# One step of a four-layer streaming encoder on one core: five plain column blocks per feed-forward, and full-height low parts of the attention queries

## The chip, the core and the metric

The kernel runs on one core of a Trainium2 chip. The metric is the device time of one execution in microseconds (us). Five engines work side by side, each on its own list of instructions: PE (TensorE, matmuls; PEld is its weight load), DVE (VectorE), ACT (ScalarE), POOL (GpSimd) and SP (which only issues DMAs here). The scheduler inside the kernel fixes the order on each engine when the program is built, so an engine waits when the next instruction on its list is not ready.

## The reference, cut to what matters

Four layers run over 576 tokens at once (512 of a prompt, 64 of a running stream), model width 1024. Each layer adds a token mixer (pool, delta rule, stick-breaking attention, pool) and then a feed-forward; this is the feed-forward and the part of attention in which the queries are used:

```python
def _conv_ffn(h, buf, w_up, conv_w, conv_b, w_down):      # D_FF = 2816
    val, gate = jnp.split(h @ w_up, 2, axis=-1)
    gate, new_buf = _causal_dwconv(gate, buf, conv_w)
    return (jax.nn.silu(gate + conv_b) * val) @ w_down, new_buf

def _sb_attend(q, k, v, q_pos, k_pos):                    # 16 heads of 64
    z = jnp.einsum('bqhd,bshd->bhqs', q, k).astype(jnp.float32) * (SB_DH ** -0.5)
    mask = k_pos[None, :] < q_pos[:, None]
    log_1m = jnp.where(mask, jax.nn.log_sigmoid(-z), 0.0)
    rest = lax.cumsum(log_1m, axis=3, reverse=True) - log_1m
    a = jnp.where(mask, jnp.exp(jax.nn.log_sigmoid(z) + rest), 0.0)
    return jnp.einsum('bqhs,bshd->bqhd', a, v.astype(jnp.float32))
```

## The kernel before, in words

**Precision.** Every 32-bit matrix is split into a rounded high part (written by ACT) and a low part, the rest (written by DVE). A product is three matmuls: high by high, high weight by low token, low weight by high token. The tokens' parts are `xh[m]`, `xl[m]` for m = 0 to 7 (128 features by 576 tokens each); weights pass from raw tiles `r` to split tiles `h` (8 of them).

**Stages.** P0 F0 D1 F1 S2 F2 P3 F3 and an ending: mixer, then feed-forward, of each layer. In the trace F0 begins near 70 us, F1 near 935, S2 near 1304, F2 near 1678, F3 near 2120.

**A feed-forward (`ffn`)** has 22 column blocks j of 128. The first `J0` (4) are plain: `up(j)` makes gate and value, each 8 k-steps by 3 products by 2 token halves of 288, so 96 matmuls of 288 columns. The others, `up2(j)`, make gate and value together as a 2 by 2 block product by seven products instead of eight (84 matmuls of 288 columns). The seven products take other operands: the tokens already normalised (`xh`, `xl` rewritten in place), and sums of token quarters, `T`. `sums(k)`, for k = 0 to 3, makes both: on DVE two multiplications, four subtractions and three low parts give T of k; then, once the event `plain` has fired (after the last plain block's matmuls), ACT rewrites `xh[k]`, `xh[k+4]` (rows `xh<-b`) and DVE `xl[k]`, `xl[k+4]` (rows `xl<-b,xh`). Block J0 waits for all four k before its first product. `splitter2` makes the seven weight combinations on DVE (rows `r<-r`) and splits them (`h<-r,h`). `down(js)` multiplies a group of finished blocks into the residual `x`: 96 matmuls for the first group of two blocks (0, 1), 192 for a group of four; its results are added by DVE (`a<-p,a`, two per output tile m). The first group's `down` is put after block `max(2, J0-1)`, thus after the last plain block and ahead of the first seven-product block.

**Attention (`sb`)**: per pair of heads `q_post` scales the queries into `t`, then writes two tiles `qa[e]` (e = 0, 1 for the two heads; the rounded queries of one head, twice, on both partition halves) and one tile `qb` (each head's low part on its own 64 partitions). The keys `k_[e]` hold a head's rounded part on its own half and its low part on the other, so one matmul over 128 partitions gives (high + low key) by high query (`sc`). Then the mask is added by bf16 matmuls against `idb` (`diag`), and `half` adds high key by low query over 64 partitions alone. Per head `attend` does this for three score tiles in the order 1, 2, 0: tile 1 has low matmuls of 384 and 128 columns, tile 2 of 256, 64, 64 and 64, tile 0 of 512. That is 7 per head, 112 in all.

**The scheduler** (`Flow.run`) is a list of generators with priorities: it always emits the next step of the most urgent one whose operands are ready by its own clocks, and keeps each engine's list in that order. Pools bound it: 25 tiles `a`, 8 `b`, 11 `d` (128 by 128, mostly for the delta rule's chain).

Of the kernel before, what the change touches and what calls it, by code (L numbers as in the profile page):

```python
# [9 lines left out]
F32 = mybir.dt.float32  # L10
F32R = mybir.dt.float32r
BF16 = mybir.dt.bfloat16
AF = mybir.ActivationFunctionType
ALU = mybir.AluOpType
# [3 lines left out]
class Eng:  # L18

    def __init__(self, flow, name, obj):  # L20
        self.flow, self.name, self.obj = flow, name, obj
# [268 lines left out]
class Step:  # L290
    def __init__(self, ctx, tc, I, O):
        self.tc=tc; nc=self.nc=tc.nc; self.I=I; self.O=O; self.n=0
        f=self.f=Flow(tc)
        self.V,self.A,self.G,self.E,self.S=f.V,f.A,f.G,f.E,f.S
        self.cp=ctx.enter_context(tc.tile_pool(name="const",bufs=1))
        self.sp=ctx.enter_context(tc.tile_pool(name="sb",bufs=1))
        self.dp=ctx.enter_context(tc.tile_pool(name="dr",bufs=1,space=bass.MemoryType.DRAM))
        self.pp=ctx.enter_context(tc.tile_pool(name="ps",bufs=1,space=PSUM))
        for tag,n in (("a",25),("b",8),("r",4),("h",8),("p",8),("q",8),("d",11)): f.slots(tag,n)
        f.slots("so",1); f.slots("t",8)  # L300
        f.lim.update(w=8,g=4,c=8,z=3,o=2,f=6)
        self.jobs=[]; self.specs=[]; self.wq={}; self.spl=[]; self.ngot=0
        self.x=[None]*KD; self.xd={}; self.rb={}; self.acc={}; self.cnt=Counter()
# [341 lines left out]
    def ffn(self,l,st,nst,gnext):  # L645
# [3 lines left out]
        cw,fst=self.fc[l]; gb=32+8*l  # L649
        act={}; ps={}  # L650
        so=[None]
        J0=4
        def conv(j,Gt,c):
            yield [Gt,"@A"]
            A.activation(c[:,:578],Gt[:,2:580],AF.Identity,bias=cw[:,66+j:67+j],scale=cw[:,44+j:45+j])
            G.tensor_copy(so[0][:,0:2,j],Gt[:,512:514]); G.tensor_copy(so[0][:,2:4,j],Gt[:,578:580])
            yield [c,"@V"]
            V.scalar_tensor_tensor(out=c[:,:578],in0=Gt[:,1:579],scalar=cw[:,22+j:23+j],in1=c[:,:578],op0=ALU.mult,op1=ALU.add)
            V.scalar_tensor_tensor(out=c[:,:578],in0=Gt[:,0:578],scalar=cw[:,j:j+1],in1=c[:,:578],op0=ALU.mult,op1=ALU.add)
# [41 lines left out]
        def up(j,stag):  # L701
            def gen():
                if j==0:
                    f.lim["g"]=6
                    yield [("so",1)]
                    so[0]=self.s([128,4,NF],F32,"so",1)
                f.spawn(post(j),10)
                need=self.xneed(st) if j==0 else None
                if stag:
                    W=[]  # L710
                    for i in (0,1): W.append((yield from self.wget()))
                    P=[[None,None],[None,None]]; ps[j,0],ps[j,1]=P
                    for h in (0,1):
                        for i in (0,1):
                            yield [("p",1,"g")]
                            P[i][h]=self.p("g")
                            yield from self.gemm(P[i],W[i][0],0,self.xk,KD,halves=(h,),need=need)
                            if h: f.free(*W[i][1])
                            f.fire(f"{st}:{'gv'[i]}{j}:{h}")
                else:  # L720
                    for i in (0,1):
                        w,hl=yield from self.wget()
                        yield [("p",2,"g")]
                        P=[self.p("g"),self.p("g")]; ps[j,i]=P
                        yield from self.gemm(P,w,0,self.xk,KD,need=need)
                        f.free(*hl)
                        for h in (0,1): f.fire(f"{st}:{'gv'[i]}{j}:{h}")
                if j==J0-1: f.fire(f"{st}:plain")
            self.job(gen,(wu[:,:,DFF+128*j:DFF+128*j+128],KD,128),(wu[:,:,128*j:128*j+128],KD,128))
# [48 lines left out]
        def frees():  # L778
            yield [f"{st}:N{k}" for k in range(4)]+[f"{st}:post{j}" for j in range(J0)]
            f.free(self.rb[st])  # L780
# [5 lines left out]
        def tok(i,k):  # L786
            if i in (1,2,4): return T[i,k][:,H0],T[i,k][:,H1]
            m,h=((k,H0),(k+4,H0),(k+4,H1),(k,H1))[(11,21,22,3).index(i)]
            return self.xh[m][:,h],self.xl[m][:,h]
# [38 lines left out]
        def up2(j):  # L828
            def gen():
                B=[None]*3  # L830
                f.spawn(post2(j,B),10)
                for n,(b,t,read) in enumerate(SEQ):
                    w,hl=yield from self.wget()
                    if read: yield [f"{st}:{read}{j}"]
                    start=B[b] is None
                    if start:
                        yield [("p",1,"g")]
                        B[b]=self.p("g")
                    o=B[b][:,:HW]
                    for k in range(4):  # L840
                        if j==J0: yield [f"{st}:{'T' if t in (1,2,4) else 'N'}{k}"]
                        xh,xl=tok(t,k)
                        yield [xh,xl]
                        wh,wl=w[0][:,k],w[1][:,k]

                        mm(o,wh,xh,start=start and k==0,stop=False,skip_group_check=not start)
                        mm(o,wh,xl,start=False,stop=False,skip_group_check=not start)
                        mm(o,wl,xh,start=False,stop=k==3,skip_group_check=not start)
                    f.free(*hl)
                    f.fire(f"{st}:P{j}:{n}")  # L850
                if j==NF-1: f.free(*T.values())
            self.job(gen,(wu[:,:,DFF+128*j:DFF+128*j+128],wu[:,:,128*j:128*j+128]))
# [48 lines left out]
        for g in groups:  # L901
            for j in g:
                if j<J0: up(j,j==0)
                else: up2(j)
                if pend is not None and j==max(g[0],J0-1): down(pend,False); pend=None
            pend=g
# [775 lines left out]
    def sb(self,l,st,nst,gnext):  # L1682
# [60 lines left out]
        HS=(slice(0,64),slice(64,128))  # L1743
# [3 lines left out]
        def q_post(p_,P):  # L1747
            rb=self.rb[st]
            yield [f"{st}:rb0",f"{st}:rb1",("a",1)]
            t=self.a()  # L1750
            for h in (0,1):
                a,b=HALF[h]
                yield [P[h][:,:HW],rb[:,a:b],"@V"]
                V.scalar_tensor_tensor(out=t[:,a:b],in0=P[h][:,:HW],scalar=0.125,in1=rb[:,a:b],op0=ALU.mult,op1=ALU.mult)
                f.free(P[h])
            yield [t,("a",3),"@A"]
            qa=[self.a(F32R),self.a(F32R)]; qb=self.a(F32R)
            for e in (0,1):
                for r in (e,1-e): A.activation(qa[e][HS[r],:NT],t[HS[e],:NT],AF.Copy)
            for e in (0,1):  # L1760
                yield [qa[e],"@V"]
                V.tensor_tensor(out=qb[HS[e],:NT],in0=t[HS[e],:NT],in1=qa[e][HS[e],:NT].bitcast(F32),op=ALU.subtract)
            f.free(t)
            qT[p_]=(qa,qb)
            f.fire(f"{st}:q{p_}")
# [42 lines left out]
        def proj(which,p_):  # L1808
            def gen():
                w,hl=yield from self.wget()  # L1810
                yield [("p",2,"g")]
                P=[self.p("g"),self.p("g")]
                yield from self.gemm(P,w,0,self.xk,KD)
                f.free(*hl)
                f.spawn((q_post,k_post)[which](p_,P),TN[('pc','pd')[which]])
            self.job(gen,(W[:,:,1024*which+128*p_:1024*which+128*p_+128],KD,128))
# [4 lines left out]
        def attend(p_,e):  # L1821
            n_=2*p_+e
            yield [f"{st}:q{p_}",f"{st}:k{p_}"]+([f"{st}:z{n_-1}"] if n_ else [])
            (qa,qb),k_,kp=qT[p_],kT[p_],kP[p_]
            hs=HS[e]; z={}; E={}; X={}; Lt={}

            def sc(*parts):
                for n,(o,kk,qs) in enumerate(parts): mm(o,kk,qa[e][:,qs],start=n==0,stop=False)
            def half(*parts):
                for n,(o,kk,qs) in enumerate(parts): mm(o,kk[hs],qb[hs,qs],start=False,stop=n==len(parts)-1)  # L1830
            def zk(b):
                i,c,n=reg[b]
                return z[i][:,c:c+n],k_[e][:,128*b:128*b+128],slice(128*b,512)
# [35 lines left out]
            def post(i):  # L1869
# [7 lines left out]
                if not left[0]:  # L1877
                    EE[p_,e]=E
                    f.fire(f"{st}:E{p_}:{e}")
            yield [qa[e],qb[hs,:NT],k_[e],kp[:,:512],self.idb,self.mkb,self.ntri,self.none]  # L1880
            for i in order:
                yield [("p",1,"z")]
                z[i]=self.p("z")
# [7 lines left out]
                half(*ps)  # L1891
                f.spawn(pre(i),TN['pe'])
            f.fire(f"{st}:z{n_}")
            if e: f.free(*qa,qb,*k_,kp)
            def Lr(b,x):
                i,c,n=reg[b]
                return X[i][x][:,c:c+n]
# [47 lines left out]
        q=lambda p_: proj(0,p_)  # L1945
        for x in TN['order2'].split(): dict(k=k,q=q,v=values)[x[0]](int(x[1:]))
        for p_ in range(8):
            for e in (0,1): f.spawn(attend(p_,e),TN['pa'])
            f.spawn(av(p_),TN['pb'])
# [88 lines left out]
```

## Time and profile before

| what | value |
|---|---|
| median of 3 runs | 2518.58 us (2518.18 to 2522.79) |
| the profiled execution, its own time | 2525.03 us |
| its span, first to last instruction | 2523.3 us |
| mean granted TensorE clock | 0.986 of full speed |
| PE busy | 2462.4 us (98%), 18337 matmuls |
| DVE, ACT, POOL busy | 1924.9 us (76%), 1298.2 us (51%), 365.9 us (15%) |

The span is nearly all PE time, so the table is read by what keeps PE from its next matmul, and by how fast it does each one. Matmuls overlap: a row's duration runs from the matmul's start to its end, and the pace is the distance from one start to the next.

### The profile page before, as it was taken

How to read it: one execution, taken by the hardware profiler on the slowest of the kernel's cores; microseconds unless marked ns; L12 is line 12 of the kernel's file. 1: busy time of each engine (PE TensorE's matmuls, PEld its weight loads, DVE VectorE, ACT ScalarE, POOL GpSimd, SP SyncE). 2: the span in 40 equal slices, each digit the busy share in tenths (PEclk: the TensorE clock that was granted, in tenths of full speed). 3: DMA queues.
4: the chain of work that ended last, by engine and by line, in shares of the span. 5: the costliest groups of instructions: out<-in, count | busy, mean ns of one | idle time of the engine just before them, and what ended most of it. 6: DMA issues, size and time to landing. Idle time of an engine off the chain costs nothing.

```text
span 2523.3 us, 46793 instructions
## 1 busy us (share of the span) xinstructions
PE 2462.4 (98%) x18337; PEld 2394.3 (95%) x18337; DVE 1924.9 (76%) x3727; ACT 1298.2 (51%) x2459; POOL 365.9 (15%) x734
## 2 busy tenths in 40 slices
PE   8989999998999999999999999999999999899998
PEld 7989999998999899999999888899999999899998
DVE  6988787887555479877885767779777788877776
ACT  6455544544344344444565667645444465544445
POOL 0000000138441001000001221200000001000000
PEclk9999999999999999999999999999999999999999
DMA  3223223332322222323233122222233231223231
GB/s 110 83 87 101 84 78 100 108 95 62 79 65 57 75 77 63 97 88 97 86 125 113 51 78 64 92 71 79 84 91 94 86 107 53 76 76 97 88 95 62
DMA packets 349056, 212.91 MB, mean 84 GB/s; under 512 B 30298, under 2 KB 341210, under 8 KB 348836
## 3 DMA queue, kind: packets, MB, share of 16 engines
q1 hardware_dynamic: 348836, 209.93, 28.3%
q8 instruction: 144, 2.36, 0.4%
q14 instruction: 76, 0.62, 0.1%
HBM read 192.41 MB, written 17.47 MB: 83 GB/s over the span
## 4 chain that ended last, share of the span: by engine, by line
PE 66%; DVE 2%; issue 1%; ACT 0%; POOL 0%; DVEq 0%; POOLq 0%; ACTq 0%
PE p L26 66%; DVE a L26 1%; DVE h L26 1%; DVE r L26 0%; ACT a L26 0%; DVE b L26 0%; ACT b L26 0%; POOL t L26 0%; DVE xl L26 0%; DVE q L26 0%; ACT xh L26 0%; DVEq L2034 0%; ACT q L26 0%; POOL rtf L26 0%; POOLq L2034 0%
## 5 line engine op out<-in xcount | busy, mean ns | idle before, releaser
L26 PE MATMUL p<-xh,h 128*128 128x288 f32 x4864 | 1040.6, 300 | 24.1 <-ACT xh L26 20.9
L26 PEld LDWEIGHTS p<-xh,h 128*128 128x128 f32 x4864 | 803.6, 189 | 31.1 <-ACT xh L26 22.2
L26 ACT ACTIVATE h<-r 128x512 fp32r<-128x512 f32 (+1 forms) x708 | 508.4, 739 | 420.1 <-PE p L26 320.9
L26 PE MATMUL p<-xl,h 128*128 128x288 f32 x2432 | 706.0, 297 | 1.6 <-DVE xl L26 1.6
L26 PE MATMUL p<-b,h 128*128 128x288 f32 x4992 | 681.0, 297 | 5.6 <-ACT b L26 3.0
L26 PEld LDWEIGHTS p<-b,h 128*128 128x128 f32 x4992 | 668.5, 189 | 9.3 <-DVE b L26 3.8
L26 DVE TENSOR_TENSOR h<-r,h 128x512 fp32r<-128x512 f32 (+1 forms) x708 | 580.7, 829 | 52.4 <-ACT h L26 51.3
L26 PEld LDWEIGHTS p<-xl,h 128*128 128x128 f32 x2432 | 461.6, 190 | 3.5 <-DVE xl L26 3.2
L26 DVE TENSOR_TENSOR a<-p,a 128x288 f32<-128x288 f32 (+6 forms) x650 | 265.8, 448 | 197.8 <-PE p L26 188.6
L26 PE MATMUL p<-a,h 128*128 128x288 f32 x2592 | 374.1, 299 | 0.0
L26 PEld LDWEIGHTS p<-a,h 128*128 128x128 f32 x2592 | 359.5, 192 | 0.0
L26 POOL COPY so<-a 128x2 f32<-128x2 f32 x176 | 100.2, 599 | 1513.5 <-DVE a L26 1513.5
L26 ACT ACTIVATE a<-a 128x512 f32<-128x512 f32 (+6 forms) x362 | 192.9, 555 | 133.8 <-DVE a L26 117.3
L26 ACT ACTIVATE q<-p 128x288 f32<-128x288 f32 x288 | 118.2, 410 | 185.3 <-PE p L26 181.5
L26 DVE SCALAR_TENSOR_TENSOR a<-a,fcw,a 128x578 f32<-128x578 f32 x176 | 144.2, 819 | 5.5
L26 DVE TENSOR_TENSOR a<-p,q 128x288 f32<-128x288 f32 (+2 forms) x216 | 70.5, 355 | 53.7 <-PE p L26 53.5
L26 ACT ACTIVATE b<-a 128x576 fp32r<-128x576 f32 x96 | 65.5, 682 | 81.7 <-DVE a L26 81.5
L26 POOL TENSOR_TENSOR a<-a,a 128x512 fp32r<-128x512 f32 (+1 forms) x64 | 67.3, 1052 | 252.5 <-DVE a L26 237.5
L26 DVE TENSOR_TENSOR r<-r 128x512 f32<-128x512 f32 x144 | 99.9, 694 | 4.3
L26 PE MATMUL p<-a,a 128*128 128x128 f32 (+10 forms) x656 | 102.8, 287 | 0.1
L26 ACT ACTIVATE xh<-a,gains 128x288 fp32r<-128x288 f32 (+2 forms) x128 | 66.3, 531 | 70.8 <-DVE a L26 70.3
L26 DVE TENSOR_TENSOR r<-r,r 128x512 f32<-128x512 f32 x144 | 99.0, 688 | 2.5
(192 smaller groups left out, 2424.7 us busy)
## 6 DMA issues: line engine op xcount, KB each, us to landing
r<-in_ffn_w_up_dram SPq DMA_DIRECT2D x176, 512.0 KB
r<-in_ffn_w_down_dram SPq DMA_DIRECT2D x80, 512.0 KB
r<-in_dn_w_in_dram SPq DMA_DIRECT2D x32, 512.0 KB
r<-in_sb_w_qkv_dram SPq DMA_DIRECT2D x24, 512.0 KB
d<-a SPq DMA_DIRECT2D x24, 288.0 KB
a<-d SPq DMA_DIRECT2D x16, 288.0 KB
r<-in_ffn_w_down_dram SPq DMA_DIRECT2D x16, 256.0 KB
r<-in_dn_w_out_dram SPq DMA_DIRECT2D x8, 512.0 KB
```

The lines of the kernel that those rows point to most:

```text
L26: r = f(*a, **k)
```

## The change

`J0` becomes 5: block 4 of each feed-forward is plain instead of seven-product, and `down` of blocks 0 and 1 moves behind it. `qb` becomes a tile per head: 64 partitions of zeros (a memset on POOL), and the low part on the other 64; `half` then runs over all 128 partitions against the whole `k_[e]`. `q_post` asks for four `a` tiles at once instead of three. The pool of `a` grows by one, that of `d` shrinks by three.

```diff
-        for tag,n in (("a",25),("b",8),("r",4),("h",8),("p",8),("q",8),("d",11)): f.slots(tag,n)
+        for tag,n in (("a",26),("b",8),("r",4),("h",8),("p",8),("q",8),("d",8)): f.slots(tag,n)
...
-        J0=4
+        J0=5
...
-            yield [t,("a",3),"@A"]
-            qa=[self.a(F32R),self.a(F32R)]; qb=self.a(F32R)
+            yield [t,("a",4),"@A"]
+            qa=[self.a(F32R),self.a(F32R)]; qb=[self.a(F32R),self.a(F32R)]
+            for e in (0,1): G.memset(qb[e][HS[1-e],:NT].bitcast(F32),0.0)
...
-                V.tensor_tensor(out=qb[HS[e],:NT],in0=t[HS[e],:NT],in1=qa[e][HS[e],:NT].bitcast(F32),op=ALU.subtract)
+                V.tensor_tensor(out=qb[e][HS[e],:NT],in0=t[HS[e],:NT],in1=qa[e][HS[e],:NT].bitcast(F32),op=ALU.subtract)
...
-                for n,(o,kk,qs) in enumerate(parts): mm(o,kk[hs],qb[hs,qs],start=False,stop=n==len(parts)-1)
+                for n,(o,kk,qs) in enumerate(parts): mm(o,kk,qb[e][:,qs],start=False,stop=n==len(parts)-1)
...
-            yield [qa[e],qb[hs,:NT],k_[e],kp[:,:512],self.idb,self.mkb,self.ntri,self.none]
+            yield [qa[e],qb[e][:,:NT],k_[e],kp[:,:512],self.idb,self.mkb,self.ntri,self.none]
...
-            if e: f.free(*qa,qb,*k_,kp)
+            if e: f.free(*qa,*qb,*k_,kp)
```

The change also moves instructions. On DVE in F0, before, around the start of the first seven-product block (`xl<-b,xh` are the rewritten tokens; b_953 and b_954 belong to k = 2 and 3, `q` and `a` to T of k = 3, h_1629 to weights):

```order
L26 TENSOR_TENSOR h_1629<-r_1421,h_1629 128x512
L26 TENSOR_TENSOR xl_81<-b_953,xh_73 128x576
L26 TENSOR_TENSOR xl_85<-b_953,xh_77 128x576
L26 TENSOR_TENSOR q_1380<-b_954 128x288
L26 TENSOR_TENSOR q_1648<-b_954,q_1380 128x288
L26 TENSOR_TENSOR a_1646<-q_1380,a_1646 128x288
L26 TENSOR_TENSOR q_1653<-b_954,q_1648 128x288
L26 TENSOR_TENSOR b_954<-b_954 128x288
L26 TENSOR_TENSOR a_1650<-q_1648,a_1650 128x288
L26 TENSOR_TENSOR a_1655<-q_1653,a_1655 128x288
L26 TENSOR_TENSOR xl_82<-b_954,xh_74 128x576
L26 TENSOR_TENSOR xl_86<-b_954,xh_78 128x576
```

These twelve stood behind all sixteen additions of `down` of blocks 0 and 1. On DVE in F0 of the change, the same place (a_1530 is block 4, a_101 the residual's tile 0):

```order
L26 TENSOR_TENSOR a_1530<-a_1529,a_547 128x512
L26 TENSOR_TENSOR a_1530<-a_1529,a_547 128x64
L26 TENSOR_TENSOR xl_79<-b_951,xh_71 128x576
L26 TENSOR_TENSOR xl_83<-b_951,xh_75 128x576
L26 TENSOR_TENSOR xl_80<-b_952,xh_72 128x576
L26 TENSOR_TENSOR xl_84<-b_952,xh_76 128x576
L26 TENSOR_TENSOR xl_81<-b_953,xh_73 128x576
L26 TENSOR_TENSOR xl_85<-b_953,xh_77 128x576
L26 TENSOR_TENSOR xl_82<-b_954,xh_74 128x576
L26 TENSOR_TENSOR xl_86<-b_954,xh_78 128x576
L26 TENSOR_TENSOR a_101<-p_1606,a_101 128x288
L26 TENSOR_TENSOR a_101<-p_1607,a_101 128x288
```

All eight rewritten low parts now stand together ahead of the first addition of that `down`, and T of k = 3 ahead of them; the same holds in F1, F2 and F3. On DVE of the change, some 15 rows further on, where `down` ends and the first seven-product block begins (a_107, a_108 are the residual's tiles 6 and 7; r_1409 and r_1480 the raw weights of block 5; h_1646, h_1756 and h_1774 the low parts of its products 0, 6 and 1):

```order
L26 TENSOR_TENSOR a_107<-p_1723,a_107 128x288
L26 TENSOR_TENSOR a_107<-p_1724,a_107 128x288
L26 TENSOR_TENSOR h_1646<-r_1409,h_1646 128x512
L26 TENSOR_TENSOR h_1756<-r_1480,h_1756 128x512
L26 TENSOR_TENSOR r_1480<-r_1480 128x512
L26 TENSOR_TENSOR a_108<-p_1739,a_108 128x288
L26 TENSOR_TENSOR r_1480<-r_1409,r_1480 128x512
L26 TENSOR_TENSOR r_1409<-r_1480,r_1409 128x512
L26 TENSOR_TENSOR h_1774<-r_1480,h_1774 128x512
```

The first low parts of the new block's weights now stand behind the additions of tiles 6 and 7.

## Rows read from the trace of the kernel before

**Rows 1.** Busy time in stretches: stretch, length, PE, PEld, DVE, ACT, POOL, clock, DMA.
```profile
70.00:131.00 61.00, 59.47 (x444) 59.13 (x442) 56.09 (x109) 26.68 (x42) 5.25 (x16) 1.00 0.26 78
...
994.00:1304.00 310.00, 309.27 (x2319) 308.95 (x2319) 250.02 (x443) 157.37 (x288) 27.66 (x70) 0.99 0.32 96
...
1480.00:1626.00 146.00, 144.80 (x1048) 127.30 (x1047) 105.44 (x180) 99.70 (x170) 36.72 (x37) 0.99 0.25 77
```

**Rows 2.** PE's waits: for whom, us in total, times, longest.
```profile
PE p L26 <- ACT xh L26: 20.9, 5, 8.5
...
PE p L26 <- DVE xl L26: 1.6, 5, 0.8
```

**Rows 3.** DVE in order of time, transitions of F0 and F1: start, us, instruction.
```profile
134.53 1.42 DVE L26 TENSOR_TENSOR xl<-b,xh 128x576 fp32r<-128x576 f32 x2
...
138.77 1.43 DVE L26 TENSOR_TENSOR xl<-b,xh 128x576 fp32r<-128x576 f32 x2
...
976.93 3.43 DVE L26 TENSOR_TENSOR xl<-b,xh 128x576 fp32r<-128x576 f32 x5
```

**Rows 4.** Groups of instructions on DVE: count, busy us, mean ns, idle before.
```profile
L26 DVE TENSOR_TENSOR h<-r,h 128x512 fp32r<-128x512 f32 x520 | 350.2, 685 | 41.1 <-ACT h L26 41.1
...
L26 DVE TENSOR_TENSOR h<-r,h 128x1024 fp32r<-128x1024 f32 x188 | 230.5, 1228 | 11.3 <-ACT h L26 10.2
L26 DVE TENSOR_TENSOR a<-p,a 128x288 f32<-128x288 f32 x488 | 203.9, 453 | 182.1 <-PE p L26 179.3
...
L26 DVE SCALAR_TENSOR_TENSOR a<-a,fcw,a 128x578 f32<-128x578 f32 x176 | 144.2, 819 | 5.5
...
L26 DVE TENSOR_TENSOR r<-r 128x512 f32<-128x512 f32 x144 | 99.9, 694 | 4.3
```

**Rows 5.** Busy time in stretches, as in rows 1: six falls of the clock.
```profile
133.60:143.80 10.20, 6.28 (x21) 5.29 (x22) 8.80 (x17) 4.77 (x11) 0.00 (x0) 0.50 0.36 104
993.70:997.20 3.50, 3.17 (x13) 2.89 (x14) 3.46 (x6) 1.83 (x4) 0.00 (x0) 0.51 0.00 0
1734.40:1741.30 6.90, 5.98 (x23) 5.66 (x24) 4.92 (x9) 4.15 (x9) 0.00 (x0) 0.51 0.11 33
2171.30:2181.60 10.30, 6.54 (x26) 6.22 (x26) 8.44 (x15) 4.71 (x9) 0.00 (x0) 0.50 0.36 102
1369.20:1372.60 3.40, 3.40 (x18) 3.40 (x18) 3.33 (x7) 2.65 (x5) 2.49 (x3) 0.50 0.00 0
1505.70:1509.20 3.50, 3.50 (x15) 3.26 (x15) 3.43 (x7) 3.37 (x7) 2.44 (x2) 0.51 0.00 0
```

**Rows 6.** PE in order of time, in the last of these falls.
```profile
1506.45 0.44 PE L26 MATMUL p<-xl,h 128*128 128x288 f32 x1
1506.69 0.44 PE L26 MATMUL p<-xh,h 128*128 128x288 f32 x1
```

**Rows 7.** PE in order of time, a stretch of score tiles in S2 (64*128: 64 partitions).
```profile
1366.28 0.26 PE L26 MATMUL p<-c_sbmaskb,idb 128*128 128x128 bf16 x2
1366.47 1.07 PE L26 MATMUL p<-a,a 64*128 64x256 f32 x5
...
1368.53 0.50 PE L26 MATMUL p<-a,a 64*128 64x384 f32 x2
1368.95 0.59 PE L26 MATMUL p<-h,xh 128*128 128x256 f32 x2
```

**Rows 8.** PE in order of time: four full-height score matmuls and the mask after them.
```profile
1515.96 0.53 PE L26 MATMUL p<-a,a 128*128 128x256 f32 x4
1516.33 0.26 PE L26 MATMUL p<-c_sbmaskb,idb 128*128 128x128 bf16 x2
```

**Rows 9.** PE in order of time, D1: a bf16 mask and the 32-bit matmul after it.
```profile
548.05 0.21 PE L26 MATMUL p<-c_dnposb,idb 128*128 128x64 bf16 x1
548.10 0.38 PE L26 MATMUL p<-xh,h 128*128 128x288 f32 x1
```

**Rows 10.** PE in order of time: the last longer wait of D1.
```profile
881.32 0.61 PE L26 MATMUL p<-b,h 128*128 128x288 f32 x1 [2.22 <-ACT b L26]
```

More of the change, by code (lines that the diff above doesn't have):

```diff
@@ L1824, in attend @@
             (qa,qb),k_,kp=qT[p_],kT[p_],kP[p_]
-            hs=HS[e]; z={}; E={}; X={}; Lt={}
+            z={}; E={}; X={}; Lt={}
             def sc(*parts):
```

## The prediction

> **What bounds the kernel now.** I read the busy times by stretch first. In the body of a feed-forward PE is busy 309.27 of 310.00 us, with 2319 matmuls [rows 1]: 0.1334 us each, and nothing else counts there. In attention (S2) PE is just as full, 144.80 of 146.00 us, but its weight load is busy only 127.30; elsewhere the two are level, so something empties PE between loads [rows 1]. DVE is the nearest rival: while a feed-forward runs its plain blocks it is busy 56.09 of 61.00 us [rows 1].
>
> Then PE's own waits. Nearly all the longer ones in the feed-forwards are for the rewritten tokens: 20.9 us on ACT's `xh` in five waits and 1.6 us on DVE's `xl` in five [rows 2]. Their place is the start of block J0: in F0 DVE writes the low parts of k = 2 at 134.53 and of k = 3 at 138.77 [rows 3], behind the additions of `down`, while PE stands. Only in F1 can one see what the work costs when it stands together: five of them in 3.43 us from 976.93, 0.67 us apart [rows 3].
>
> Then the granted clock. It falls from 2.4 to 1.2 GHz around each of these four waits; PE issues 21, 13, 23 and 26 matmuls in those stretches [rows 5]. At the lower level a 288-column matmul follows the last after 0.24 us [rows 6] instead of 0.1334. Two more falls lie in S2, at 1369.2 and 1505.7 [rows 5], each right after score tiles with their 64-partition matmuls (the matmuls before the first: [rows 7]).
>
> **The change, part by part.** The sum is made against the profiled execution, 2525.03 us, which is 6.45 above the median of the runs.
>
> 1. *Block 4 plain.* 96 matmuls for 84, in four feed-forwards: 48 x 0.1334 [rows 1] = **+6.4 us**. All of it is on PE, thus on the path.
>
> 2. *The waits at the transition.* The extra block gives PE 12.8 us (96 x 0.1334) before `down`. On DVE the block costs about two weight splits of 1.228, three additions' worth of gate scaling and two of value at 0.453, two convolution steps of 0.819, and some 1.8 for the rest: 8 us [rows 4]. Dropping the seven-product weights of one block (seven splits at 0.685, four sums at 0.694) takes 7.6 away later [rows 4]. So some 5 us of DVE are free before `plain`; k = 3 needs about that (134.53 to 138.77 held all of its nine instructions [rows 3]), and in the change's order they stand there. After `plain`, eight low parts at 0.67 are 5.4 us, and `down` of blocks 0 and 1 covers them with 96 matmuls, 12.8 us. All 20.9 + 1.6 go: **-22.5 us** [rows 2].
>
> 3. *What is late next.* The new block's first weights. DVE can add tile 6 only once PE has made it, and PE then has tile 7 left, 12 x 0.1334 = 1.6 us, before it reaches the new block. In the order shown, between tile 6 and the low part of product 1 stand two additions, two splits, a sum, an addition, two sums and that split: 3 x 0.453 + 3 x 0.685 + 3 x 0.694 = 5.5 us, about 4.9 with the overlap of neighbours [rows 4]. That ends 3.4 us after PE reaches the block, and 0.25 more until PE sees it (my allowance); PE wants it after product 0 and two matmuls, 14 x 0.1334 = 1.9 us. So about 1.8 us of wait in each of four transitions: **+7.2 us**. Bounds: 0, if ACT and DVE get ahead, and twice that.
>
> 4. *The clock at the transition.* 83 matmuls ran at the low level; each gave up 0.24 - 0.133 = 0.107 us: **-8.9 us** [rows 5, 6]. A wait of 1.8 us is shorter than what stood at those falls (22.5 us over four transitions is 5.6 each [rows 2]), but not nothing, so I let two of four keep the shortest fall seen there, 13 matmuls, 1.5 us each: **+3.0 us**; bounds 0 and 6.
>
> 5. *Low parts over 128 partitions.* From the first mask at 1366.28 to 1368.95 PE works through the low parts of tile 2, high and low of tile 0 and of tile 1, and five masks: 2.67 us [rows 7]. The same without emptying PE: four times 512 columns at the feed-forward's rate (0.1334 x 512/288 = 0.237) is 0.95; tile 2's four matmuls took 0.37 where nothing switched [rows 8]; masks about 0.06 each, as 0.05 passed between a mask and a 32-bit matmul in D1 [rows 9], 0.30. Together 1.62, so 1.05 a head; I take 1.0, since a weight load may bind before the 64-column ones. The arithmetic is unchanged (zeros meet the other half of the keys), and a 64-row matmul is not shorter than a full one of its width: 0.42 us to the next start after 1368.53's pair is already more than the 0.237. 16 heads: **-16.0 us**. The low bound: the mask of D1 [rows 9] stands for the step from bf16 to 32-bit at full height; if that step drained too, half the drains would stay, -8. The high bound adds the open weight load of the matmul after each low part, -18.
>
> 6. *The clock in S2.* The two falls cover 3.4 and 3.5 us [rows 5] and follow stretches thinned by those drains; denser, I expect neither: **-3.0 us**; bounds 0 and -3.5.
>
> 7. *The rest at nothing.* 16 zero fills go to POOL, busy 36.72 of 146.00 us there [rows 1]; they stand ahead of the split of a pair's queries. If that cover failed, each would hold back the queries by no more than a DVE pass over 128x576 takes, 0.67 us [rows 3], 11 in all. DMAs are the same in number and size. A pair now holds one more `a` tile, and the pool has one more. The order on PE in S2 keeps its fillers between heads; in D1 it is the same to about 680 us and then differs. There, with three `d` tiles fewer, I take 0, with a bound of 4 either way: the last wait of D1 is 2.22 us [rows 10], and in the new order more output matmuls stand before it.
>
> Sum: 6.4 - 22.5 + 7.2 - 8.9 + 3.0 - 16.0 - 3.0 = **-33.8 us**. The profiled execution would take 2491.2; from the median, 2518.58 - 33.8 = **2484.8 us**.
>
> The Trainium skill has a rule that speaks against part 5. Its page "TensorE: Matmul & The Clock Gate", section Part 3, says that a weight load overlaps a matmul in flight only when the two use different row groups; by it the 64-row form is the one that hides its load, and full height would show it. The feed-forward's 0.1334 us pace at full height [rows 1] shows loads hidden, and the trace so far disagrees; what the rule would make of the time is rival C.
>
> **Rivals.**
>
> A. *The wait moves rather than shrinks*: product 1, or a split ahead of it, costs twice my 1.8 us and all four falls stay. For it: DVE at 56 of 61 us [rows 1]. Against: the new order's eight rows together. -33.8 + 7.2 + 3.0 = -23.6: 2495.0.
>
> B. *The drain belongs to the change of number format as well*: half of part 5 and both falls in S2 stay. Against it: the 0.05 us between D1's mask and its neighbour [rows 9]. -33.8 + 8.0 + 3.0 = -22.8: 2495.8.
>
> C. *Full-height loads show*: each of the 112 low matmuls exposes some 0.11 us of load, +12.3 in place of -16.0 and -3.0. -33.8 + 31.3 = -2.5: 2516.1, no change. Against it: the pace at full height [rows 1, 8].
>
> D. *The transition keeps its waits* (the change does not do what it says): what is late is not the rewritten tokens but DVE as a whole, and it is late by as much after the extra block. Then only 1, 5 and 6 count: 6.4 - 19.0 = -12.6: 2506.0. Against it: DVE gains 5 us on PE in the block.
>
> E. *Slower: attention runs out of `a` tiles.* Four at once are asked for while heads hold theirs for up to three score tiles; the queries then come late, and each head's chain (three ACT functions, DVE, POOL) lies open instead of under another projection. The nearest prices of such a wait are D1's 2.22 us on ACT's `b` [rows 10] and the mean of the five on `xh`, 20.9/5 = 4.2 [rows 2]; in their middle, 3.2 us a head, it is 51.2 us, less 33.8: +17.4, 2536.0. It decides from 33.8/16 = 2.1 us a head. For it: one tile more asked for per pair, one in the pool for all. Against it: S2 now waits 1.2 us in 146 [rows 1], and fillers stand between the heads in the new order.
>
> **How the numbers follow.** Chances: the forecast 0.61, A 0.15, B 0.11, D 0.05, C 0.04, E 0.04. 0.2% is 5 us, about what a measurement of this kernel can tell from no change. Faster: forecast, A, B and D, 0.92; same: C, 0.04; slower: E, 0.04. The likeliest is 2484.8. Range: down by the unexposed low ends (3: 7.2, 4: 3.0, 5: 2.0, 7: 3) to about 2470, since not all fall together; up past A and B, and part of both, to 2503. C, D and E stay outside, 0.13.
>
> **What would show it.** Right: PE's waits on `xh` and `xl` near zero in the transitions, with some 2 us on DVE's `h` instead; no falls of the clock at 1369 and 1506, and two at most, short, at the transitions; no 64*128 rows in S2 but full-height ones with the next start 0.24 us on for 512 columns; the weight load in S2 nearly as busy as PE; the feed-forward pace still 0.133 us. Wrong: waits on `xh` above 5 us, an idle PE between heads in S2, 128-row low parts that start as late after the mask as the 64-row ones, or D1 longer by more than 4 us.

## The result, and the profile after

The changed kernel took **2487.51 us** (median of 4, 2486.88 to 2490.01) against 2520.64 us of the kernel before in the same session: ratio 0.9871, 95% interval 0.9854 to 0.9888, thus 33.1 us faster. The forecast was 2484.8 us in a range of 2470 to 2503, and -33.8 us as a sum. The changed kernel's mean granted clock was 0.995. A second session gave 2486.96 against 2522.51 (ratio 0.9860, 0.9845 to 0.9875). The gain came out nearly to the microsecond; the terms did not, so that closeness is in part luck, and the rest of this document is about that.

PE's waits over the whole changed kernel, for whom, us in total, times, longest:

```profile
PE p L26 <- DVE b L26: 9.3, 9, 5.9
PE p L26 <- DVE h L26: 8.4, 7, 3.2
...
PE p L26 <- ACT b L26: 3.1, 4, 1.4
```

The two lines of [rows 2], 20.9 us on `xh` and 1.6 on `xl`, have no counterpart: PE waits for the rewritten tokens nowhere. DVE's `h` has gone from 4.1 to 8.4 us: 3.9 us of the 8.4 lie at the four transitions, where part 3 put them, and 1.2 us in S2. DVE around the transition of F0 in the changed kernel, in order of time:

```profile
127.23 5.43 DVE L26 TENSOR_TENSOR xl<-b,xh 128x576 fp32r<-128x576 f32 x8
132.58 3.19 DVE L26 TENSOR_TENSOR a<-p,a 128x288 f32<-128x288 f32 x8
...
142.43 0.45 DVE L26 TENSOR_TENSOR a<-p,a 128x288 f32<-128x288 f32 x1
142.80 1.41 DVE L26 TENSOR_TENSOR r<-r,r 128x512 f32<-128x512 f32 x2
144.12 0.69 DVE L26 TENSOR_TENSOR h<-r,h 128x512 fp32r<-128x512 f32 x1
```

The eight low parts stand together and take 5.43 us, against 1.42 and 1.43 for scattered pairs in [rows 3]. The low part of product 1 ends at 144.81. PE at the same place:

```profile
141.30 0.30 PE L26 MATMUL p<-xh,h 128*128 128x288 f32 x1
...
143.29 0.53 PE L26 MATMUL p<-a,h 128*128 128x288 f32 x2 [0.24 <-ACT h L26]
144.87 0.93 PE L26 MATMUL p<-a,h 128*128 128x288 f32 x5 [1.04 <-DVE h L26]
```

PE reaches the new block at 141.30 without a pause, makes product 0 and waits at product 1: 0.24 us for ACT, 1.04 for DVE. F1 and F2 have 1.04 for DVE as well, F3 0.76.

The body of F1, and S2, in stretches (stretch, length, PE, PEld, DVE, ACT, POOL, clock, DMA), which answer to [rows 1]:

```profile
995.00:1289.00 294.00, 294.00 (x2216) 293.88 (x2214) 235.80 (x418) 148.15 (x269) 26.16 (x66) 1.00 0.32 96
1289.67:1601.85 312.18, 307.93 (x2373) 286.31 (x2373) 231.25 (x410) 214.84 (x375) 77.55 (x82) 1.00 0.28 84
```

The pace in F1 is 294.00/2216 = 0.1327 us a matmul, as before. S2 took 322.79 us in the kernel before and 312.18 now, with the same 2373 matmuls and a granted clock of 1.00. PE now stands (length less PE's busy time) 4.25 us in it, where it stood 1.06 before. Below, a fall of the clock is a stretch in which the granted clock reads 0.50, that is 1.2 instead of 2.4 GHz.

To see where the time went I cut each profile at the same matmuls: those that start behind the wait at the end of P0, of F0, of D1, of F1, of S2, of F2 and of F3 (in the kernel before at 61.78, 448.97, 881.32, 1302.67, 1625.46, 2046.30 and 2485.82). Lengths in us, F1 with D1's output projection, F3 with P3:

| kernel | F0 | D1 | F1 | S2 | F2 | F3 |
|---|---|---|---|---|---|---|
| before | 387.2 | 432.4 | 421.4 | 322.8 | 420.8 | 439.5 |
| before, second profile | 387.0 | 433.0 | 422.4 | 321.5 | 418.4 | 438.9 |
| changed | 379.6 | 430.2 | 418.9 | 312.2 | 417.0 | 429.8 |
| changed, second profile | 380.2 | 430.1 | 417.4 | 312.9 | 416.9 | 429.8 |

By the sum, the four feed-forwards should have given 14.8 us, S2 19.0 and D1 nothing. In the means of these rows the feed-forwards gave 23.0, S2 9.6 and D1 2.6. Two errors of opposite sign, 8 to 9 us each, met: that the total fits is luck.

### The profile page after: what moved, and what is told of

The parts are those of the page before. It is cut to its first block, busy times and chain, and to the rows that moved or that the text cites. A ratio compares the mean times of both kernels' runs of the same rounds, so it can differ in the third digit from the quotient of the medians.

```text
span 2486.1 us, 46793 instructions
## 1 busy us (share of the span) xinstructions
PE 2440.4 (98%) x18385; PEld 2381.6 (96%) x18385; DVE 1904.6 (77%) x3695; ACT 1282.5 (52%) x2419; POOL 373.1 (15%) x750
## 4 chain that ended last, share of the span: by engine, by line
PE 88%; DVE 4%; issue 3%; POOL 3%; DMA 1%; ACT 1%; SPq 0%; DVEq 0%; POOLq 0%; ACTq 0%
PE p L26 88%; DVE a L26 2%; DVE h L26 1%; POOL h L26 1%; POOL q L26 1%; ACT a L26 1%; DMA b<-in_x_prompt_dram 0%; DVE r L26 0%; DVE b L26 0%; POOL a L26 0%; DMA a<-in_cache_sb_k_dram 0%; ACT b L26 0%; POOL t L26 0%; POOL dn_so L26 0%; SPq L26 0%
## 5 line engine op out<-in xcount | busy, mean ns | idle before, releaser
L26 PE MATMUL p<-xh,h 128*128 128x288 f32 x4992 | 1061.5, 300 | 4.6 <-DVE h L26 4.4
L26 PEld LDWEIGHTS p<-xh,h 128*128 128x128 f32 x4992 | 820.9, 189 | 10.1 <-DVE h L26 4.8
L26 PE MATMUL p<-xl,h 128*128 128x288 f32 x2496 | 720.3, 296 | 0.0
L26 PEld LDWEIGHTS p<-xl,h 128*128 128x128 f32 x2496 | 472.8, 189 | 0.5
L26 DVE TENSOR_TENSOR a<-p,a 128x288 f32<-128x288 f32 (+4 forms) x662 | 269.5, 446 | 204.9 <-PE p L26 190.7
L26 PE MATMUL p<-a,h 128*128 128x288 f32 x2448 | 347.6, 295 | 4.6 <-DVE h L26 3.9
L26 PEld LDWEIGHTS p<-a,h 128*128 128x128 f32 x2448 | 331.8, 188 | 6.3 <-DVE h L26 4.8
L26 ACT ACTIVATE a<-a 128x512 f32<-128x512 f32 (+7 forms) x358 | 192.4, 559 | 130.6 <-DVE a L26 109.9
L26 ACT ACTIVATE a<-p 128x448 f32<-128x448 f32 (+5 forms) x149 | 64.8, 454 | 71.7 <-PE p L26 54.4
L26 PE MATMUL p<-a,a 128*128 128x128 f32 (+6 forms) x656 | 94.4, 284 | 1.1 <-ACT b L26 0.8
```

Source lines behind the costliest of these rows:

```text
L26: r = f(*a, **k)
```

## The experiments

There are twelve runs, in three sessions. The kernel before ran in each of them, with medians of 2519.39, 2522.46 and 2522.51 us, and each ratio is against the one of the same session. Stage lengths come from one profiled execution of each run.

### The kernel before, a second profile

No edit.

> The kernel before, a second time, to see which of its waits repeat. Theory: the profiled execution was some 4 us longer than the median because the waits on xh and xl at the starts of block J0 vary from one execution to the next (8.49 us in F3 that time, 4.50 and 2.61 in F0); here their sum should come out 3 to 6 us below 22.5 and the span near 2519 us. Rival: the waits are fixed by the order of instructions and repeat within 1 us, and the 4 us lie elsewhere.

2521.17 us, span 2519.4. The long waits at the starts of block 4 repeat to 0.01 us (4.49, 0.76 and 2.61 in F0, 8.49 in F3), so the rival holds: they are set by the order. The 3.9 us of span by which the profile read before the prediction was longer lie mainly in P0 (1.0), S2 (1.3) and F2 (2.4), the last two with one fall of the clock more each. Falls of the clock are not fixed: this execution has one in S2, at 1402, and none at F2's transition.

### The two parts alone, and the pools undone

Block 4 alone, on the kernel before:

```diff
-        J0=4
+        J0=5
```

> Block 4 plain and nothing else: the queries' low parts and the pools as before. Theory (the two parts of the change add up, and the feed-forwards gave more than forecast, attention less): 20 to 23 us faster, about 2499 us; waits on xh and xl gone, about 4.4 us of waits on h in their place, none of the four falls of the clock there; S2 stays at 322 to 323 us with its two falls. Rival (the sizes of the prediction): 14.8 us faster, about 2506 us.

2499.56 us, ratio 0.9917 (0.9903 to 0.9932): 19.8 us faster. That is just under the theory's 20 to 23, and well over the rival's 14.8; the waits and the falls at the transitions went as the theory said. S2 stays at 322.7 us with two falls of the clock.

The other parts alone, on the changed kernel:

```diff
-        J0=5
+        J0=4
```

> Full-height low parts and the new pools, with four plain blocks as before. Theory: 10 to 12 us faster than before, about 2509 us, S2 at 312 us: the score matmuls of S2 take 36.6 us in place of 48.7, both falls of the clock in S2 are gone, and some 2.5 us of new waits in S2 are in it; the transitions keep their waits and falls. Rival (the sizes of the prediction): 19 us faster, about 2502 us.

2512.69 us, ratio 0.9970 (0.9958 to 0.9982): only 6.7 us faster, less than either expected (its profiled execution, 2511.42, is 9.8 under the second profile of the kernel before). S2 is 312.0 us and has no fall, as the theory said. The four transitions keep their waits and their falls, and F0 is 2.0 us longer. So the parts do not add up: 19.8 and 6.7 us are 26.5, where both together gave 33.1. F0 holds 2 us of the difference; the rest is not placed, and the kernel before itself moved by 3 us between sessions.

The changed kernel with the old pools:

```diff
-        for tag,n in (("a",26),("b",8),("r",4),("h",8),("p",8),("q",8),("d",8)): f.slots(tag,n)
+        for tag,n in (("a",25),("b",8),("r",4),("h",8),("p",8),("q",8),("d",11)): f.slots(tag,n)
```

> The changed kernel with the pools of before (25 a, 11 d). Theory: pools are worth nothing, 2487 us within 2 us; D1 stays at 430 us and S2 at 312. Rival 1: the new waits in S2 come from a tiles being short; with one fewer they grow, S2 above 314. Rival 2: fewer d tiles are what made D1 2.2 us shorter (another order of its end); then D1 is back at 432.

2508.24 us, ratio 0.9951 (0.9935 to 0.9968). **The pools, which the sum had at nothing, are worth 21 us** in the kernel with full-height low parts. S2 takes 336.1 us: rival 1.

```profile
1291.70:1627.80 336.10, 323.46 (x2373) 298.87 (x2373) 232.93 (x409) 216.06 (x375) 76.41 (x82) 0.94 0.26 80
```

D1 takes 432.8 us, and its last wait is 2.22 us again, as in [rows 10], where the changed kernel has 1.37: rival 2 too.

### Which pool

The changed kernel with one `a` tile fewer and `d` as changed (`("a",25)`, `("d",8)`):

> The changed kernel with 25 a tiles and 8 d tiles. With 25 and 11 it was 21 us slower, all of it in S2 (336 us in place of 312). Theory (the one a tile is what attention runs short of): S2 at 334 to 338 us, 2508 us. Rival (the three d tiles, or the order that they set, did it): S2 at 312 us, 2487 us. D1 should stay at 430 us in either case if the d tiles set its end, and be at 432 if the a tile does.

2506.17 us, ratio 0.9941 (0.9926 to 0.9956). S2 330.7 us, D1 430.2: the `a` tile decides S2, the `d` tiles D1. PE stands 12.64 us in S2 here and 12.64 with the old pools, so the 5.4 us between the two are the clock's, and the profile with the old pools is of the slowest of its four executions (2513.34). D1 was 429.6 to 431.3 us in nine profiles with 8 `d` tiles, 431.6 to 433.0 in four with 11. What an `a` tile fewer does is seen first at 1440. Three stretches of this kernel, the whole of S2, S2 up to there and the next 30 us, as above:

```profile
1288.90:1619.60 330.70, 318.06 (x2373) 293.69 (x2373) 233.08 (x410) 216.01 (x375) 76.55 (x82) 0.97 0.26 81
1288.90:1440.00 151.10, 151.09 (x1175) 143.85 (x1175) 110.73 (x203) 98.65 (x176) 29.88 (x32) 1.00 0.27 84
1440.00:1470.00 30.00, 23.74 (x118) 18.81 (x118) 21.89 (x38) 21.30 (x35) 9.47 (x10) 0.72 0.24 73
```

The same 30 us of the changed kernel:

```profile
1440.00:1470.00 30.00, 30.00 (x236) 28.06 (x236) 25.99 (x43) 25.66 (x46) 9.42 (x10) 1.00 0.43 128
```

Half the matmuls (118 for 236), at a mean clock of 0.72. What PE waited for there, in the kernel with 25: DVE, then ACT, then PE, in order of time:

```profile
1440.47 0.82 DVE L26 SCALAR_TENSOR_TENSOR a<-p,a 128x288 f32<-128x288 f32 x2
```

```profile
1441.38 2.80 ACT L26 ACTIVATE a<-a 64x576 fp32r<-64x576 f32 x4 [0.16 <-DVE a L26]
```

```profile
1442.83 0.79 PE L26 MATMUL p<-a,a 128*128 128x384 f32 x2 [2.78 <-ACT a L26]
```

The first is `q_post` scaling a pair's queries; the second makes the two `qa`; the third is the first score matmul of that pair, 2.78 us late. In the changed kernel the same pair's queries are scaled, and its first score matmul starts, at

```profile
1443.10 0.81 DVE L26 SCALAR_TENSOR_TENSOR a<-p,a 128x288 f32<-128x288 f32 x2
```

```profile
1447.34 0.40 PE L26 MATMUL p<-a,a 128*128 128x384 f32 x2
```

so 4.24 us apart in place of 2.36, and PE does not wait. That is rival E of the prediction: the queries come late, and nothing lies over them. But it is only one of the eight pairs; the other seven start their scores without a wait. After it the waits go on inside the heads, 1.44 and 1.51 us for DVE in the next 18 us, and the clock falls three times. Over the whole of S2 the 18.5 us are two things of about one size: PE stands 8.4 us more (12.64 by 4.25), and four falls, 20.4 us long together, cost up to some 10 us (half of their length, my estimate).

Five plain blocks with the new pools, the queries' low parts as before:

```diff
-        for tag,n in (("a",25),("b",8),("r",4),("h",8),("p",8),("q",8),("d",11)): f.slots(tag,n)
+        for tag,n in (("a",26),("b",8),("r",4),("h",8),("p",8),("q",8),("d",8)): f.slots(tag,n)
...
-        J0=4
+        J0=5
```

> Five plain blocks with the queries' low parts as before (64 partitions, one tile a pair) and the new pools (26 a, 8 d): against the run with five plain blocks and the old pools (2499.6 us; S2 322.7, D1 431.6). Theory (the a tile is needed only because the full-height form holds one more a pair, and the d tiles change the order at the end of D1): S2 within 1.5 us of 322, D1 near 430, time about 2498. Rival (S2 was already short of a tiles before the change, so part of its gain is the tile's): S2 below 320.

2492.35 us, ratio 0.9885 (0.9868 to 0.9901), and the changed kernel beside it 2486.96. I had expected 2498; S2 below 320 is what the rival said. S2 in this kernel and, below it, in the one with five plain blocks and the old pools, with its two falls:

```profile
1286.16:1604.59 318.43, 317.59 (x2373) 288.91 (x2374) 231.69 (x410) 215.86 (x375) 67.58 (x66) 1.00 0.26 79
```

```profile
1290.30:1613.00 322.70, 321.67 (x2373) 292.26 (x2373) 232.34 (x410) 216.42 (x375) 67.62 (x66) 0.99 0.27 83
1388.80:1392.20 3.40, 3.40 (x15) 3.16 (x15) 3.37 (x6) 3.27 (x7) 2.39 (x2) 0.50 0.42 124
1525.30:1528.70 3.40, 3.40 (x15) 3.40 (x16) 3.37 (x6) 3.27 (x7) 2.42 (x2) 0.50 0.50 149
```

The score matmuls take the same (48.4 us for 304, from each start to the next, by 48.7). Of the 4.3 us between them 3.4 are the two falls of the clock (half of twice 3.40 us), which are gone though the 64-row matmuls are all still there. D1 gave 1.6, and F1 2.2, where a fall of 6.8 us behind D1's last wait is gone. So with the new pools the full-height low parts are worth only 5.4 us (2492.35 to 2486.96, S2 318.4 to 312.9); with the old ones they cost 8.7 (2499.56 to 2508.24).

One `a` tile more than the change has (each 592 columns wide, to make room):

> The changed kernel with 27 a tiles (each 592 columns wide in place of 608, the columns left out being unused). Theory (the step from 26 to 27 still frees some of the 2.5 us of new waits in S2, nothing like the 18.5 us from 25 to 26): S2 at 310 to 312 us, 0 to 2 us faster than the changed kernel. Rival (the new waits are DVE's and ACT's work behind a faster PE): S2 unchanged within 0.5 us.

2493.68 us, ratio 0.9884 (0.9869 to 0.9899), slower than the changed kernel by 6.7 us. S2 takes 319.3 us: PE waits 1.74 us on a copy by ACT, 1.70 on another, 1.02 on POOL, and the clock falls twice. Both the theory and its rival fail. The order that the scheduler emits in S2 changes with each tile, and 26 is not a point on a line: 25, 26 and 27 gave S2 at 331 to 336, 312 and 319 us.

### What the masks cost

The score matmuls of S2 (304, from each start to the next) took 48.71 us before and 36.59 in the changed kernel: 12.1 less, where part 5 had 16.0. PE in order of time for one head of the changed kernel and the next one's first tile:

```profile
1352.32 0.26 PE L26 MATMUL p<-c_sbmaskb,idb 128*128 128x128 bf16 x2
1352.42 0.93 PE L26 MATMUL p<-a,a 128*128 128x256 f32 x5
1353.19 0.23 PE L26 MATMUL p<-c_sbmaskb,idb 128*128 128x128 bf16 x1
1353.23 0.71 PE L26 MATMUL p<-a,a 128*128 128x512 f32 x3
1353.79 0.28 PE L26 MATMUL p<-c_sbmaskb,idb 128*128 128x128 bf16 x2
1353.88 0.48 PE L26 MATMUL p<-a,a 128*128 128x384 f32 x2
1354.19 0.33 PE L26 MATMUL p<-h,xh 128*128 128x256 f32 x1
```

From the first mask of tile 2 to the matmul after the low part of tile 1 it is 1.87 us, by 2.67 in [rows 7] and 1.62 forecast. Every low part now follows the mask at once (0.03 to 0.04 us) but then holds PE about 0.08 us longer than its columns ask for (means over the 16 heads: 0.315 us for 512 columns, by 0.237 at the feed-forward's rate). The kernel before shows it too, one row behind those of [rows 9]:

```profile
548.31 0.29 PE L26 MATMUL p<-xl,h 128*128 128x288 f32 x1
```

From 548.10 to 548.31 is 0.21 us where a 288-column matmul takes 0.133. I had read the start behind the mask, 0.05 later, and not the one behind that. Is it the change of format, or the weight load? All masks in fp32r, with one `d` tile fewer to make room:

```diff
-        for tag,n in (("a",26),("b",8),("r",4),("h",8),("p",8),("q",8),("d",8)): f.slots(tag,n)
+        for tag,n in (("a",26),("b",8),("r",4),("h",8),("p",8),("q",8),("d",7)): f.slots(tag,n)
...
-self.mkb=bf("c_sbmask",[128,192])
+self.mkb=bf("c_sbmask",[128,192],F32R); self.idf=self.c([128,128],F32R,"idf")
...
-                mm(z[i][:,c:c+128],self.idb,self.mkb[:,0:128],start=False,stop=False)
+                mm(z[i][:,c:c+128],self.idf,self.mkb[:,0:128],start=False,stop=False)
...
-                if i==2: mm(z[2][:,384:448],self.idb,self.mkb[:,128:192],start=False,stop=False)
+                if i==2: mm(z[2][:,384:448],self.idf,self.mkb[:,128:192],start=False,stop=False)
```

> The changed kernel with the attention's mask matmuls in fp32r in place of bf16 (same number, same columns; one d tile fewer to make room, which can move D1 by 1 or 2 us). In the changed kernel the score matmuls of S2 took 36.6 us, about 0.08 us a mask group more than the sum allowed for. Theory (a weight load in 32 bits takes 0.11 us and a matmul of 128 columns, 0.06 us, is too short to hide it): the masks' own loads now show too, about 0.13 us a head more, score matmuls near 38.7 us, time 2 us longer or unclear. Rival (the change of number format itself costs the 0.08): three changes a head are gone, score matmuls near 33 us, time some 3 us shorter.

2494.44 us, ratio 0.9891 (0.9876 to 0.9905), some 7 us slower than the changed kernel. The score matmuls take 40.0 us without PE's waits, 3.4 more: the load, and more of it than I gave. D1, with the 7 `d` tiles, has 433.1 us and its 2.2 us wait again, so it is the order that the number sets, not fewer tiles as such. One group of that kernel:

```profile
1352.37 0.39 PE L26 MATMUL p<-c_sbmaskb,idf 128*128 128x128 f32 x2
1352.59 0.88 PE L26 MATMUL p<-a,a 128*128 128x384 f32 x6
```

Two masks now take 0.22 us from their start to the next, 0.11 each, where the bf16 pair at 1353.79 takes 0.09. No change of format is left and the cost has grown. The changed kernel settles it without a mask: the last matmul of its row at 1352.42, by itself, is a high part of 512 columns behind a 64-column score matmul, both in 32 bits.

```profile
1352.87 0.48 PE L26 MATMUL p<-a,a 128*128 128x512 f32 x1
```

The mask behind it starts at 1353.19, 0.32 us on, the same 0.08 above 0.237 with no change of format. So that rival is out: what costs is a 32-bit load behind a matmul that is shorter than the load.

Masks of a head together at its end. This run stands on the kernel with 27 `a` tiles above, not on the changed one, so it has to be compared with that (some lines left out):

```diff
-        for tag,n in (("a",26),("b",8),("r",4),("h",8),("p",8),("q",8),("d",8)): f.slots(tag,n)
+        for tag,n in (("a",27),("b",8),("r",4),("h",8),("p",8),("q",8),("d",8)): f.slots(tag,n)
...
                 sc(*ps)
-                for b in ((0,),(1,3),(2,))[i]: diag(b)
-                if i==2: mm(z[2][:,384:448],self.idb,self.mkb[:,128:192],start=False,stop=False)
                 half(*ps)
+            for i in order:
+                for b in ((0,),(1,3),(2,))[i]: diag(b,b in (0,3))
+                if i==2: mm(z[2][:,384:448],self.idb,self.mkb[:,128:192],start=False,stop=True)
                 f.spawn(pre(i),TN['pe'])
...
```

> The changed kernel with the five mask matmuls of a head after all its score matmuls, high and low, so that two of three steps from a short mask to a 32-bit load are gone per head. Theory (the load of 0.11 us behind a matmul too short to hide it, some 0.05 us each): score matmuls of S2 at 35 us in place of 36.6; the time the same within what can be told, since the score tiles are then ready up to 1 us later. Rival (the 0.05 is not the load's): 36.6 us.

2497.98 us, ratio 0.9905 (0.9890 to 0.9920): slower than the changed kernel by 11 us, but 6.7 of them are the 27th tile's, so 4.3 are the masks'. The score matmuls took 35.9 us, 0.7 less, half of what I expected. Only tile 0's low part is freed by it (0.236 us for its 512 columns); those of tiles 1 and 2 now stand behind high parts of 128 and 64 columns, which are as short as the mask. The scores come later, and S2 waits 12.9 us (one of 3.27 on DVE) and takes 324.9, where the kernel with 27 tiles waits 6.9 and takes 319.3. A small saving on PE was paid back several times by the order.

### The transition

The `down` of blocks 0 and 1 ahead of the last plain block:

```diff
-                if pend is not None and j==max(g[0],J0-1): down(pend,False); pend=None
+                if pend is not None and j==max(g[0],J0-2): down(pend,False); pend=None
```

> The changed kernel with the down of blocks 0 and 1 put ahead of the last plain block (4) in place of behind it. Theory (DVE's lead makes T in time, but it is this down that covers the eight low parts after the last plain block): PE waits 5 to 6 us on xh and xl at each of the four transitions, and the clock falls there again; 20 to 30 us slower than the changed kernel, about 2512 us. Rival (the extra block alone gives DVE the time): no waits on xh and xl above 1 us, 2487 us within 3.

2493.29 us, ratio 0.9891 (0.9875 to 0.9908); its profiled execution, the fastest of four, took 2489.64. My theory fails by far. ACT and DVE, then PE, at F0's transition of this kernel:

```profile
137.02 4.69 ACT L26 ACTIVATE xh<-b 128x576 fp32r<-128x576 f32 x8
```

```profile
137.90 5.43 DVE L26 TENSOR_TENSOR xl<-b,xh 128x576 fp32r<-128x576 f32 x8
```

```profile
139.19 0.43 PE L26 MATMUL p<-xh,h 128*128 128x288 f32 x2
140.04 0.40 PE L26 MATMUL p<-xl,h 128*128 128x288 f32 x1 [0.42 <-DVE xl L26]
140.28 0.43 PE L26 MATMUL p<-xh,h 128*128 128x288 f32 x2
141.38 0.40 PE L26 MATMUL p<-xl,h 128*128 128x288 f32 x1 [0.67 <-DVE xl L26]
141.61 0.42 PE L26 MATMUL p<-xh,h 128*128 128x288 f32 x2
142.72 0.40 PE L26 MATMUL p<-xl,h 128*128 128x288 f32 x1 [0.68 <-DVE xl L26]
```

The rewriting begins at 137.02, 2.2 us ahead of the new block: in the kernel's code the last plain product reads the eight feature blocks one after the other, so each can be rewritten once that product is past it. What nothing covers is 0.42 + 0.67 + 0.68 = 1.77 us, and no wait on `h` follows. In all PE waits 7.1 us on `xl` in place of 4.6 on `h`: DVE's lead removes most of the old waits. The cover of `down` is worth 2.5 us by these waits and 6.3 by the medians (2493.29 to 2486.96).

Six plain blocks (`J0=6`):

> The changed kernel with six plain blocks. Theory (after the fifth, a further plain block buys nothing: the waits on xh are gone, and the 1.0 us on h at product 1 comes from the order behind the down, not from too little time): the price of the first term alone, 48 x 0.1334 = 6.4 us slower, 2494 us, with the waits on h as they are. Rival (the lead of DVE still counts): the waits on h go as well, 4.4 us less, 2489 to 2490 us.

2495.87 us, ratio 0.9898 (0.9883 to 0.9913): 26.6 us faster than before, where the change gave 33.1 and 35.6 in its two sessions, so 6.5 to 9 slower. The 6.4 of part 1 is the low end of that, and the waits on DVE's `h` are 1.04 us in all four transitions. The theory holds.

The changed kernel once more, for the comparisons above:

> The changed kernel again, beside the others on one chip: 2487 us, S2 at 312 us, no falls of the clock in S2 or at the transitions.

2486.96 us; S2 312.9, no falls of the clock in S2 or at a transition. No version I ran beats the changed kernel.

## Why the prediction came out right, step by step

Measured means the two profiled executions. Their spans differ by 4 us more than the medians, because that of the kernel before was a slow one (2525.03 us).

| step | forecast, us | measured, us | from |
|---|---|---|---|
| 1 block 4 plain | +6.4 | +6.4 | the pace; the sixth block's 6.5 to 9 |
| 2 waits on xh, xl | -22.5 | -22.5 | none left in the waits |
| 3 new wait on product 1 | +7.2 | +4.6 | DVE 1.04, 1.04, 1.04, 0.76; ACT 0.24, 0.27, 0.25 |
| 4 clock at the transition | -8.9 | -8.9 | no fall at any |
| 4 falls that stay | +3.0 | 0 | the same |
| 5 full-height low parts | -16.0 | -12.1 | 304 score matmuls |
| 6 clock in S2 | -3.0 | -3.5 | other projections, 198.2 to 194.7 |
| 7 waits in S2 | 0 | +3.2 | PE's standing time in S2, 1.06 to 4.25 |
| 7 rest of S2 | 0 | +1.6 | cumulative sums and value matmuls |
| 7 D1 and its fall | 0 | -3.9 | D1 -2.2; F1, from a 6.8 us fall to one of 3.4, -1.7 |
| sum | -33.8 | -35.1 | the spans differ by 37.2, 0.8 of it in P0, 1.3 not placed |

**Step 2** was right in its size. Its reason was half right: T of k = 3 is made in time, as forecast. That `down` has to cover all 5.4 us of low parts was wrong: the run without that cover left 1.77 us of them bare at a transition.

**Steps 3 and 4** were mis-sized. The chain on DVE was the one named, and it ended 3.5 us after PE reached the block, against the 3.4 + 0.25 of the sum (4.9 less 1.6 is 3.3; the slip is small). But product 0 and the two matmuls are followed by the wait on ACT's `h`, and PE stood 1.28 us in place of 1.8. The allowance for falls of the clock was not needed: in ten profiles with these waits, 40 transitions, not one has a fall.

**Step 5** failed in one number, the 0.06 us a mask from [rows 9]. Three times a head a 32-bit load follows a mask, and 16 x 3 x 0.08 = 3.8 us is nearly the 3.9 that was missing. That is rival B in a milder form, though not by the number format. Rival C is out: in the low parts a load showed behind the masks, three times a head, and not at each of the seven matmuls. The Trainium skill's page "TensorE: Matmul & The Clock Gate", section Part 3, on which it rested, has a weight load overlap only where row groups differ; the 0.133 us pace and the 12.1 us gained here disagree. Nor did that rule make the 64-row form the one that hides its load, as the prediction read it: all low matmuls of a head use the same 64 rows, and the high ones all 128.

**Step 6** had the right size, and its reason is not shown. One profile with all the 64-row matmuls and the new pools had no fall in S2 either, and one of the kernel before had one in place of two. Whether the pools or chance did that, single profiles do not settle. The mean granted clocks of four executions each point to the pools: 0.995 to 0.997 with them and the 64-row matmuls, 0.993 to 0.995 with the old ones, 0.994 to 0.996 in the changed kernel beside it. They hold the falls of the other stages too, so it stays open.

**Step 7** is where the prediction was weakest. "A pair now holds one more `a` tile, and the pool has one more" was put at nothing, and no row stood behind that. It came out small because the change carries the one tile that it needs; without the new pools it would have taken 2508 us, outside the stated range. Rival E, with 0.04, named the mechanism, and its 51 us of cost were 18 to 24 when it was provoked, about half of it by the clock. The 3.2 us of new waits in S2 are the mild form that stayed. With 8 `d` tiles D1 became shorter, within the 4 us of the bound.

## What to carry to other kernels

Price a pool's size like an operation: build the neighbours (one tile fewer, one more) and look at the stage that uses it, because in an order emitted by a scheduler a saving on PE of 0.7 us came with 5.6 us more in the stage. When two parts are summed, compare the sum stage by stage after the run; a total within 1 us may be two errors of 9. To price a short matmul, read the start after the next one, since its cost falls on the instruction behind it.

## What the runs showed of the hardware that I had not expected

A 32-bit weight load holds PE for about 0.11 us behind a matmul that is shorter than that: two 32-bit masks of 128 columns held PE for 0.22 us, two bf16 ones for 0.09, the 288-column matmul behind a 64-column bf16 mask took 0.21 us in place of 0.133, and the 512-column one behind a 64-column 32-bit matmul 0.32 in place of 0.237.

The clock behind D1's last wait: after 2.22 us it fell in all five profiles with that wait, after 1.37 us in four of the nine others. At F2's transition, after 2.65 and 2.66 us, it fell in one of the two profiles of the kernel before. Behind the waits of a transition in the ten profiles with `down` behind the last plain block (at most 1.04 us at a time for DVE) it never fell, and in the run with waits of 0.42, 0.67 and 0.68 us close together it fell at one transition of four.
